# Pair sums and gated products carried across FFN tiles, and three convolution parts issued later in the mix

## The chip, the cores and the metric

The kernel runs on one core of one Trainium2 chip, as one launch. The metric is the device time of that launch in microseconds. The time before is the median of three runs.

A core has engines that run side by side, each with a queue of its own that it works through in order: PE (TensorE, the matrix multiplier), DVE (VectorE), ACT (ScalarE), POOL (GpSimd) and SP (SyncE), which here issues the loads of the weights. Matmul results land in PSUM, and DVE or ACT take them from there to SBUF. An instruction that waits for another engine holds up all that stand behind it in its own queue.

## What is computed

The reference is one inference step of a decoder trunk of two layers, for a prompt of 512 tokens and 8 samples of one token each. The kernel holds all 520 tokens as columns. Cut to what matters:

```python
def swiglu_ffn(x, wg, wu, wd):
    return (jax.nn.silu(x @ wg) * (x @ wu)) @ wd          # 1024 -> 2816 -> 1024

def layer(x, ...):
    x = x + 0.5 * swiglu_ffn(rms_norm(x, ffn1_norm), ffn1_wg, ffn1_wu, ffn1_wd)
    h = rms_norm(x, mix_norm)
    z = h @ w_in                                           # split into the inputs below
    o_r = rms_norm(retention(rq, rk, rv, ret_s), ret_norm_g) * jax.nn.silu(rg)   # 4 heads
    o_a = swa_attention(q, k, v, ...)                      # 4 query heads, window 128, sinks
    o_c = conformer_conv(ca, cg, conv_buf, ...)            # taps, layer norm, silu, then y @ pw
    x = x + jnp.concatenate([o_r, o_a, o_c], axis=-1) @ w_out
    x = x + 0.5 * swiglu_ffn(rms_norm(x, ffn2_norm), ffn2_wg, ffn2_wu, ffn2_wd)
    return x, ...                                          # and the new states and windows
```

## The kernel before

**Products in two parts.** A float32 value is kept as a high part and a low part in PE's float32r format. ACT makes the high part by a copy (`split_hi`, L290), DVE the low part by a subtraction (`split_lo`, L296), and each product is three matmuls (L334 and L342): high by low, high by high, low by high.

**The FFN.** The 2816 hidden channels are 22 tiles of 128. For each tile the gate product and the up product are formed over all 1024 inputs, then `gated` takes Silu of the gate half (L434) and multiplies (L436). There are two ways to form a tile:

- A *chunk* tile (`hidden`): 16 groups of matmuls (L342) with the weights as they are. DVE scales the gate half (L448) and the up half (L454).
- A *paired* tile (`pair_hidden`, the numbers in PAIRED): a fast multiplication scheme of two-by-two blocks, with seven block products (a11, s1, s2, a12, s3, s4, a22) in place of eight. `seven` issues them, 12 matmuls each (L334: four blocks, three matmuls for each). Products s1, s2 and s4 need sums of weight blocks, which DVE forms in place (`sums`: L258 for s1, L260 and L261 for s2, L263 for s4), into two slots of the tile Rd. Between products ACT copies an accumulator to the place where the next product adds to it: L528 copies c22 after a11, and product s2 waits for it.

The down projections are formed for groups of hidden tiles: group 0 (tiles 0 to 7) after hidden tile 8, group 1 (tiles 8 to 15) after hidden tile 16, group 2 (16 to 21) at the end. Groups 0 and 1 use the paired scheme (`pair_down`), whose right-hand sides are two hidden tiles and four sums of their halves: `pair_blocks` copies and splits the halves (ACT L509, DVE L512 three times), forms the four sums (`sums4`, DVE L461 to L464), copies them (ACT L480 twice) and splits them (DVE L484 twice).

**What sets the order.** All queues are filled in program order. The work of `gated`, `pair_blocks` and the other generators goes into a list `waiting`; `advance` runs the next piece, up to its `yield`. `seven` calls it after each product, seven times for a tile, and `hidden` after every second group, eight times. `flush` runs all that is left; it is called after every hidden tile and before each down projection. The weights come through four raw buffers of 512 KB; `load` issues the next DMA on SP when a buffer is free, which is when the last split of its products is done. `ahead` runs before each product: it makes casts as far ahead as the buffers of the split weights reach, then the subtractions, and after a product (not after a chunk) the sums of the next two products.

**The mix.** Its steps (input projection tiles, retention, attention, convolution, output projection) are generators as well, and a table ORDER written out by hand says which of them makes its next step. `cv` is the convolution: its last three steps are the product with pw (24 matmuls in two halves, into two PSUM tiles), the two high parts (ACT L774) and the two low parts (DVE L777). `n0` to `n3` are the norms of the four retention heads (column sums on PE L361, ACT L375 to L377, DVE L379, L380 and L1162), `g0` to `g3` the products with their gates (DVE L1178, split by ACT L1181 and DVE L1183), `s0` to `s3` the attention blocks of the prompt (scores on PE L867, DVE L852, ACT L879 to L888, transposes on PE L894, the copy L899, the product L906), `sa` the attention of the samples (PE L934). `kv` updates the retention state (PE L1051). The output projection (L342 again) follows.

PSUM is one pool of four tiles; each `ptile()` takes the next, and its first matmul waits until the last reader of the tile's previous content is done:

```python
    psum = pool("psum", 4, space=bass.MemoryType.PSUM)
```

Of the kernel before, what the change touches and what calls it, by code (L numbers as in the profile page):

```python
# [87 lines left out]

ORDER = """
CG0 al nrm h nrm pw l nrm pw h nrm l nrm CG0 rd RK0 CG0 CA0 h RK0 l CA1 CA0 h CG0 t l t t t CG1 t h t l t t t t CA1 t  # L90
RV1 h CG1 t CG1 l t t t t RV2 h t t RV1 l t t t t RV3 t RV1 h t RV2 l t t t t t RK1 h l t RV3 RV2 t ts ts RV1 RK1 t h
l RV2 RV1 RK1 RK1 RV2 RQ0 RK1 CG1 t t t t RQ0 t t h t l t t t t RQ1 RV3 RV0 h RQ1 qr l t t t t t RG0 t h t RV0 l t t t
RG0 t t RV0 AQ0 h t RG0 l t t t t AQ1 h AQ0 l t t RV0 h RV3 AQ1 RV3 RV0 t ri2 t AQ1 rv ri0 rv AQ1 RK0 cv ri0 AQ0 AQ0
rl AK0 AQ1 cv ri2 AQ1 rs0 cv RK0 rs0 AQ1 l h rs1 AV0 l rs1 AK0 AK0 RG1 h AK0 AV0 l AV0 rm RG1 h RG1 l AQ0 rm rm cv AQ0
RG2 AQ0 cv qs cv RG3 h RG2 cv l RG2 cv h RG3 AV0 RG3 cv AV0 RK0 kv cv kv cv kv AK0 l AK0 ri2 AK0 AK0 ri0 ri2 s1 ri0 n0
n2 s1 n1 n0 n3 s0 n3 n2 s0 n0 n1 n0 s3 s1 g0 n2 s1 n1 n2 g0 s1 n1 g2 n3 g1 s1 g1 g0 n3 g3 s0 s1 sa s2 g2 s3 g1 g3 s3
s1 s1 g2 g3 s0 s0 s1 sa a0 s3 s3 s2 a1 sa a0 s2 sa a2 a1 h s2 s2 l s3 a2 a3 s3 sa s3 a3 h sa s0 l s3 sa s0 s3 s0 sa s0
s2 a4 s0 s2 a5 a4 a6 a5 sa h s2 a6 a7 s2 s2 b0 l h l b1 b0 b0 b1 b0 b0 b2 h b0 b1 b1 b2 b1 b2 b1 b2 b3 l b4 h b3 b3 l
b2 b3 b5 b4 b3 b2 b4 b3 b4 b6 h b5 b5 l b4 b5 b7 a7 b6 b5 b4 b5 b6 b6 b7 b6 b7 b6 b7 b7 b7
""".split()  # L100


# [34 lines left out]
def step_kernel(ctx: ExitStack, tc: tile.TileContext, io: dict):  # L137
# [66 lines left out]
    seq, slot = [], [0]  # L204
# [14 lines left out]
    chunk = [0]  # L219
# [95 lines left out]
    def next_tile(look=True):
        u, c = at
# [122 lines left out]
    def hidden(norm, first):  # L439

        og, ou = ptile(), ptile()
        for i, (o, k) in enumerate(ffn_tiles(first, og, ou)):
            mm3(o, next_tile(), xh[:, k], xl[:, k], k == 0, k == KD - 1)
            if i % 2:
                advance()
            if i + 1 == KD and not first:
                t = wt("t")
                nc.vector.tensor_mul(v2(t), og[:, :, :HN], v2(R))  # L448
        if first:
            run(norm)  # L450
# [3 lines left out]
        nc.vector.tensor_mul(v2(u), ou[:, :, :HN], v2(R))  # L454
        return t, u, None
# [19 lines left out]

    def sum_parts(th, tl, u, w):
        sums4(u, w)
        yield
        for i, src in enumerate((u, w)):
            nc.scalar.copy(th[:, i * NT : (i + 1) * NT], src)  # L480
# [18 lines left out]
    def pair_blocks(u, w, spare, hs):  # L499
# [81 lines left out]
    def ffn(l, name, norm, after):  # L581
        hs, even, spare, xs = {n: [] for n in range(len(GROUPS))}, None, [], []
        for step, n in ffn_steps():
            if step == "hidden":
                g = next(i for i, (a, b, _) in enumerate(GROUPS) if a <= n < b)
                t, u, v = pair_hidden(xs) if n in PAIRED else hidden(norm, n == 0)
                flush()
                waiting.append(gated(t, u, v))
                if GROUPS[g][2] and n % 2:
                    waiting.append(pair_blocks(even, u, spare, hs[g]))  # L590
# [3 lines left out]
                    waiting.append(two_parts(u, hs[g]))  # L594
                waiting.extend(input_sums(l, name, j, xs) for j in {0: (0,), 1: (1, 2), 2: (3,)}.get(n, ()))
                continue
            flush()
            if GROUPS[n][2]:
                for m in range(0, KD, 2):
                    pair_down(m, hs[n])  # L600
# [833 lines left out]
```

## Time and profile before

| | |
|---|---|
| median of 3 runs | 1906.71 us (1905.59 to 1906.8) |
| the profiled execution | 1903.99 us |
| its span, first to last instruction | 1902.2 us |
| mean granted PE clock | 0.989 |
| matmuls | 15182 |
| loads of weights (512 KB each) | 318, 3.6 us from issue to landing (median) |

All views are of the one profiled execution. A row of a timeline gives the start in us from the span's start, the duration, the engine, the line, the operation and its tiles, and in brackets how long the engine was idle before it and what it waited for. A row of the waits gives the same for all instructions of a line: total us, how often, the longest. A line with `x12` joins as many like instructions. PE's granted clock is 1.00 at full speed.

### The profile page before, as it was taken

Reading aid. Unit: us, or ns where it says so; the run is one execution under the profiler, and the core shown is the slowest. Engines: PE = TensorE matmul, PEld = TensorE weight load, DVE = VectorE, ACT = ScalarE, POOL = GpSimd, SP = SyncE. Lnnn points to the kernel's source line nnn. Section 1 sums busy time; section 2 is a strip of 40 time slices with the busy share of each in tenths; the row PEclk is TensorE's granted clock in tenths of the full one; section 3 lists DMA queues with packets and bytes.
Section 4 is the critical chain, followed back from the end, with each engine's and each line's share of the span. In section 5 each row is a group of like instructions: output and inputs, shape, how many; then the busy total and the mean of one; then the engine's idle time right before and its main releaser. Section 6 shows DMA issues by size and latency. Waiting matters only on the chain.

```text
span 1902.2 us, 37220 instructions
## 1 busy us (share of the span) xinstructions
PE 1845.5 (97%) x15182; PEld 1821.8 (96%) x15182; DVE 1552.9 (82%) x2587; ACT 1051.3 (55%) x2052; POOL 23.3 (1%) x52
## 2 busy tenths in 40 slices
PE   8999999999999999999999999999998999999999
PEld 8999999999989999999999999999998999999999
DVE  8988888688667989888779888876886579889984
ACT  6655646533765656645555556565237556466452
POOL 0000000000100000000000000000000000000000
PEclk9999999999999999999999999999999999999999
DMA  5233224433312233323323232434333132333332
GB/s 182 79 100 112 90 89 127 129 104 115 117 43 92 78 90 100 102 88 107 116 80 100 87 92 89 124 114 125 101 113 105 45 100 68 95 108 100 92 96 90
DMA packets 54173, 189.37 MB, mean 100 GB/s; under 512 B 6273, under 2 KB 7153, under 8 KB 54001
## 3 DMA queue, kind: packets, MB, share of 16 engines
q1 hardware_dynamic: 50784, 177.35, 30.8%
q0 software_dynamic: 3072, 9.53, 1.5%
q8 instruction: 119, 1.95, 0.4%
q14 instruction: 54, 0.43, 0.1%
q10 hardware_dynamic: 144, 0.11, 0.0%
HBM read 179.50 MB, written 7.45 MB: 98 GB/s over the span
## 4 chain that ended last, share of the span: by engine, by line
PE 68%; DVE 20%; ACT 5%; issue 4%; DMA 3%; DVEq 0%; ACTq 0%; POOL 0%; POOLq 0%
PE o L342 37%; PE o L334 29%; DVE wl L296 4%; DVE wh L296 3%; DMA w<-in_w 2%; DVE m L484 2%; DVE u L436 1%; DVE m L512 1%; DVE u L431 1%; DVE w L260 1%; DVE t L431 1%; DVE t L429 1%; PE o L361 1%; ACT wh L290 1%; DVE u L462 1%
## 5 line engine op out<-in xcount | busy, mean ns | idle before, releaser
L342 PE MATMUL o<-xl,wh 128*128 128x260 f32 x1920 | 389.8, 284 | 6.5 <-DVE xl L387 6.0
L342 PE MATMUL o<-xh,wl 128*128 128x260 f32 x1920 | 387.6, 284 | 0.9 <-DVE wl L296 0.9
L342 PE MATMUL o<-xh,wh 128*128 128x260 f32 x1920 | 387.4, 283 | 0.0
L334 PE MATMUL o<-m,wh 128*128 128x260 f32 x2592 | 352.9, 286 | 16.8 <-ACT o L528 15.5
L290 ACT CAST wh<-w 128x1024 fp32r<-128x1024 f32 (+1 forms) x318 | 261.4, 822 | 193.3 <-PE o L342 134.9
L334 PE MATMUL o<-m,wl 128*128 128x260 f32 x2592 | 352.4, 285 | 16.2 <-ACT o L528 15.1
L334 PEld LDWEIGHTS o<-m,wh 128*128 128x128 f32 x2592 | 330.3, 191 | 20.9 <-ACT o L528 18.5
L334 PEld LDWEIGHTS o<-m,wl 128*128 128x128 f32 x2592 | 329.5, 190 | 20.0 <-ACT o L528 17.9
L342 PEld LDWEIGHTS o<-xl,wh 128*128 128x128 f32 x1920 | 297.4, 189 | 7.8 <-ACT wh L355 5.9
L342 PEld LDWEIGHTS o<-xh,wl 128*128 128x128 f32 x1920 | 297.1, 189 | 1.1 <-DVE wl L296 1.1
L342 PEld LDWEIGHTS o<-xh,wh 128*128 128x128 f32 x1920 | 296.6, 189 | 0.0
L296 DVE TENSOR_TENSOR wl<-w,wh 128x1024 fp32r<-128x1024 f32 x150 | 183.3, 1222 | 45.3 <-ACT wh L290 40.0
L342 PE MATMUL o<-m,wh 128*128 128x260 f32 x1024 | 164.5, 282 | 1.7 <-DVE m L520 1.7
L342 PEld LDWEIGHTS o<-m,wh 128*128 128x128 f32 x1024 | 140.0, 188 | 2.5 <-DVE m L520 2.5
L296 DVE TENSOR_TENSOR wh<-w,wh 128x512 fp32r<-128x512 f32 x168 | 115.1, 685 | 8.8 <-ACT wh L290 8.8
L296 DVE TENSOR_TENSOR wl<-w,wl 128x512 fp32r<-128x512 f32 x168 | 115.1, 685 | 8.7 <-ACT wl L290 8.7
L290 ACT CAST wl<-w 128x512 fp32r<-128x512 f32 x168 | 104.3, 621 | 30.0 <-PE o L334 16.1
L334 PE MATMUL o<-xh,wl 128*128 128x260 f32 x624 | 115.8, 283 | 0.0
L334 PE MATMUL o<-xh,wh 128*128 128x260 f32 x624 | 115.5, 282 | 0.0
L290 ACT CAST wl<-Rd 128x512 fp32r<-128x512 f32 x126 | 78.5, 623 | 59.6 <-PE o L334 27.8
L290 ACT CAST wh<-Rd 128x512 fp32r<-128x512 f32 x126 | 78.5, 623 | 57.5 <-PE o L334 26.3
L342 PE MATMUL o<-m,wl 128*128 128x260 f32 x512 | 102.7, 282 | 0.0
(219 smaller groups left out, 2674.7 us busy)
## 6 DMA issues: line engine op xcount, KB each, us to landing
w<-in_w SPq DMA_DIRECT2D x318, 512.0 KB, 3.6
out_y<-x SPq DMA_DIRECT2D x8, 260.0 KB, 2.0
m<-in_cm POOLq DMA_DIRECT2D x4, 512.0 KB, 4.2
m<-in_s_ret SPq DMA_DIRECT2D x4, 512.0 KB, 5.7
m<-sc POOLq DMA_DIRECT2D x8, 256.0 KB, 4.4
out_o_rets<-m POOLq DMA_DIRECT2D x4, 512.0 KB, 3.5
x<-in_x SPq DMA_DIRECT2D x3, 520.0 KB, 6.8
w<-in_w SPq DMA_DIRECT2D x4, 256.0 KB, 4.9
```

The costliest lines, as they stand in the source:

```text
L260: nc.vector.tensor_sub(a21, a21, a11)
L290: nc.scalar.copy(spl[u][0], source(u))
L296: nc.vector.tensor_sub(lo, source(u), h.bitcast(F32))
L334: nc.tensor.matmul(o, lhsT=a[:, s], rhs=b, start=first and j == 0 and i == 0, stop=j == JP - 1 and i == 2, skip_group_check=True,)
L342: nc.tensor.matmul(o[:, s, :HN], lhsT=a, rhs=b[:, s * HN : (s + 1) * HN], start=first and i == 0, stop=last and i == 2,)
L361: nc.tensor.matmul(o[:, s, :HN], lhsT=w, rhs=v[:, s * HN : (s + 1) * HN], start=i == 0, stop=i == len(parts) - 1,)
L429: nc.vector.tensor_add(d[:, HN:], d[:, HN:], v)
L431: nc.vector.tensor_mul(d, d, R)
L436: nc.vector.tensor_mul(u, u, t)
L462: nc.vector.tensor_sub(b12, b12, b11)
L484: nc.vector.tensor_sub(tl[:, c], src, th[:, c].bitcast(F32))
L512: nc.vector.tensor_sub(lo, a, h.bitcast(F32))
```

## The change

Four parts; nothing is removed from the computation and no instruction is added, only their order in the queues changes.

1. `ffn`: `flush` after a hidden tile is called only for tiles below the first paired one. What is left in `waiting` then goes on in the next tile. Before a paired down projection all but the last generator (the `gated` of the newest tile, which that projection doesn't use) are flushed; the last is put back and goes on during the projection.
2. `hidden`: `advance` is called after every group of matmuls, not every second, as long as more than two generators wait.
3. `pair_blocks` and `sum_parts`: an extra `yield` ahead of `sums4` and one behind it, so the work takes six calls instead of four.
4. `ahead`: after a product the sums are made for up to three of the next products, stopping at a pair of raw buffers that isn't loaded yet, and at an s1 while an s4 waits for its split, since both use slot 0 of Rd.

And in the mix the last three `cv` steps stand later in ORDER, among the steps of the norms and of the attention.

```diff
@@ ORDER (lines left out stand as they are) @@
-RG2 AQ0 cv qs cv RG3 h RG2 cv l RG2 cv h RG3 AV0 RG3 cv AV0 RK0 kv cv kv cv kv AK0 l AK0 ri2 AK0 AK0 ri0 ri2 s1 ri0 n0
+AQ0 cv qs cv RG3 h RG2 cv l RG2 cv h RG3 AV0 RG3 AV0 RK0 kv kv kv AK0 l AK0 ri2 AK0 AK0 ri0 ri2 s1 ri0 n0 n2 s1 n1 n0
+n3 s0 n3 n2 s0 n0 n1 n0 s3 s1 g0 n2 s1 n1 n2 g0 s1 n1 cv g2 n3 g1 s1 g1 cv g0 n3 g3 cv s0 s1 sa s2 g2 s3 g1 g3 s3 s1 s1
...
@@ def ahead @@
             split_lo()
         else:
             split_lo(old)
-            sums(nxt[0])
-            sums(nxt[0] + 1)
+            for v in range(nxt[0], min(nxt[0] + 3, len(seq))):
+
+                load()
+                if seq[v][0] != "chunk" and seq[v][1] + 1 >= loaded[0]:
+                    break
+                if seq[v][0] == "s1" and any(seq[p][0] == "s4" for p in pending):
+                    break
+                sums(v)
@@ def hidden @@
             mm3(o, next_tile(), xh[:, k], xl[:, k], k == 0, k == KD - 1)
-            if i % 2:
+            if i % 2 or len(waiting) > 2:
                 advance()
@@ def sum_parts @@
         sums4(u, w)
         yield
+        yield
         for i, src in enumerate((u, w)):
@@ def pair_blocks @@
         for (h, lo), a in zip(b, src):
             nc.vector.tensor_sub(lo, a, h.bitcast(F32))
+        yield
         yield from sum_parts(th, tl, u, w)
@@ def ffn @@
                 t, u, v = pair_hidden(xs) if n in PAIRED else hidden(norm, n == 0)
-                flush()
+                if n < PAIRED[0]:
+                    flush()
                 waiting.append(gated(t, u, v))
...
+            rest = [waiting.pop()] if GROUPS[n][2] else []
             flush()
+            waiting.extend(rest)
             if GROUPS[n][2]:
                 for m in range(0, KD, 2):
                     pair_down(m, hs[n])
```

Lines of the changed kernel lie a few further down, by 6 to 11: L460, L467 to L470, L491 and L442 are L454, L461 to L464, L484 and L436 of before; L385, L788, L863, L878, L905 and L945 are L379, L777, L852, L867, L894 and L934.

The queue of DVE at the end of hidden tile 8, first FFN, where the first down projection begins. Before:

```order
L464 TENSOR_TENSOR u<-u 128x260
L484 TENSOR_TENSOR m<-u,m 128x520 x2
L454 TENSOR_TENSOR u<-o,R 128x520
L436 TENSOR_TENSOR u<-u,t 128x520
L263 TENSOR_TENSOR Rd<-w,Rd 128x512
L296 TENSOR_TENSOR wl<-w,wl 128x512
L296 TENSOR_TENSOR wh<-Rd,wh 128x512
L258 TENSOR_TENSOR Rd<-w 128x512
```

And in the changed kernel, from the same sum on:

```order
L470 TENSOR_TENSOR u<-u 128x260
L460 TENSOR_TENSOR u<-o,R 128x520
L491 TENSOR_TENSOR m<-u,m 128x520 x2
L263 TENSOR_TENSOR Rd<-w,Rd 128x512
L296 TENSOR_TENSOR wl<-w,wl 128x512
L296 TENSOR_TENSOR wh<-Rd,wh 128x512
L258 TENSOR_TENSOR Rd<-w 128x512
L260 TENSOR_TENSOR w<-w 128x512
L261 TENSOR_TENSOR Rd<-w 128x512
L442 TENSOR_TENSOR u<-u,t 128x520
```

The scaling of the up half comes before the splits of the pair sums, and the gated product of the tile (L436, now L442) goes behind the next sums L258 to L261; L263 has one operation less in front of it since the sums.

The same queue at the end of hidden tile 12, where paired tile 13 begins. Before:

```order
L464 TENSOR_TENSOR u<-u 128x260
L484 TENSOR_TENSOR m<-u,m 128x520 x2
L454 TENSOR_TENSOR u<-o,R 128x520
L263 TENSOR_TENSOR Rd<-w,Rd 128x512
L296 TENSOR_TENSOR wh<-w,wh 128x512
L296 TENSOR_TENSOR wl<-Rd,wl 128x512
L258 TENSOR_TENSOR Rd<-w 128x512
L436 TENSOR_TENSOR u<-u,t 128x520
```

In the changed kernel:

```order
L470 TENSOR_TENSOR u<-u 128x260
L460 TENSOR_TENSOR u<-o,R 128x520
L263 TENSOR_TENSOR Rd<-w,Rd 128x512
L491 TENSOR_TENSOR m<-u,m 128x520 x2
L296 TENSOR_TENSOR wh<-w,wh 128x512
L296 TENSOR_TENSOR wl<-Rd,wl 128x512
L258 TENSOR_TENSOR Rd<-w 128x512
L260 TENSOR_TENSOR w<-w 128x512
L261 TENSOR_TENSOR Rd<-w 128x512
```

Here L263 passes the two splits of the pair sums (L484, now L491) as well.

The queue of PE in the mix of layer 0, from the column sums of the norms to the output projection; the numbers tell the PSUM tiles `o` apart. Before:

```order
L361 MATMUL o_6192<-rsq_6184,one128_118 128x260 x2
L361 MATMUL o_6195<-rsq_6171,one128_118 128x260 x2
L361 MATMUL o_6210<-rsq_6179,one128_118 128x260 x2
L867 MATMUL o_6217<-m_6141,m_5718 128x256 x4
L894 MATMUL o_6261<-cc_85,m_6173 128x128 x8
L934 MATMUL o_6285<-m_4602,m_4606 32x128 x8
L867 MATMUL o_6295<-m_6141,m_5718 128x256 x4
```

In the changed kernel, where o_6221 and o_6234 are the two halves of the product with pw:

```order
L367 MATMUL o_6160<-rsq_6152,one128_118 128x260 x2
L367 MATMUL o_6163<-rsq_6139,one128_118 128x260 x2
L367 MATMUL o_6178<-rsq_6147,one128_118 128x260 x2
L878 MATMUL o_6185<-m_6109,m_5718 128x256 x4
L348 MATMUL o_6221<-m_6014,pwh_4549 128x260 x2
...
L348 MATMUL o_6234<-m_6013,pwl_4550 128x260 x2
L905 MATMUL o_6255<-cc_85,m_6141 128x128 x8
L945 MATMUL o_6285<-m_4602,m_4606 32x128 x8
L878 MATMUL o_6295<-m_6109,m_5718 128x256 x4
```

The pw product now stands between the last scores and the transposes; in the program before it stood ahead of L1051. The queue of DVE at the same place, from the fourth norm on, before:

```order
L379 SCALAR_TENSOR_TENSOR nt_6256<-o_6192,epst_86,nt_6256 128x520
L380 SCALAR_TENSOR_TENSOR rr_6254<-nt_6256,y0_6255 128x520
L1162 SCALAR_TENSOR_TENSOR m_5879<-m_5879,par_84,rr_6254 128x520
L1178 TENSOR_TENSOR m_6011<-m_6011,m_5879 128x520
L852 ISA m_6301,st_6216<-o_6217,m_4164,nsink_120 128x256
```

In the changed kernel:

```order
L385 SCALAR_TENSOR_TENSOR nt_6250<-o_6160,epst_86,nt_6250 128x520
L386 SCALAR_TENSOR_TENSOR rr_6248<-nt_6250,y0_6249 128x520
L1173 SCALAR_TENSOR_TENSOR m_5879<-m_5879,par_84,rr_6248 128x520
L1189 TENSOR_TENSOR m_6011<-m_6011,m_5879 128x520
L788 TENSOR_TENSOR m_6266<-o_6221,m_6265 128x520
L788 TENSOR_TENSOR m_6266<-o_6234,m_6265 128x520
L863 ISA m_6301,st_6184<-o_6185,m_4164,nsink_120 128x256
```

The two low parts of the pw product (L777, now L788) stand behind the fourth norm's gate product and ahead of the last scores' reduction, and they are the last readers of the PSUM tiles o_6221 and o_6234.

More of the change, by code (lines that the diff above doesn't have):

```diff
@@ L90 @@
 CG0 al nrm h nrm pw l nrm pw h nrm l nrm CG0 rd RK0 CG0 CA0 h RK0 l CA1 CA0 h CG0 t l t t t CG1 t h t l t t t t CA1 t
[L91 to L94, printed above, removed]
-RG2 AQ0 cv qs cv RG3 h RG2 cv l RG2 cv h RG3 AV0 RG3 cv AV0 RK0 kv cv kv cv kv AK0 l AK0 ri2 AK0 AK0 ri0 ri2 s1 ri0 n0
[L96 to L99, printed above, removed]
+RV1 h CG1 t CG1 l t t t t RV2 h t t RV1 l t t t t RV3 t RV1 h t RV2 l t t t t t RK1 h l t RV3 RV2 t ts ts RV1 RK1 t h l
+RV2 RV1 RK1 RK1 RV2 RQ0 RK1 CG1 t t t t RQ0 t t h t l t t t t RQ1 RV3 RV0 h RQ1 qr l t t t t t RG0 t h t RV0 l t t t
+RG0 t t RV0 AQ0 h t RG0 l t t t t AQ1 h AQ0 l t t RV0 h RV3 AQ1 RV3 RV0 t ri2 t AQ1 rv ri0 rv AQ1 RK0 cv ri0 AQ0 AQ0 rl
+AK0 AQ1 cv ri2 AQ1 rs0 cv RK0 rs0 AQ1 l h rs1 AV0 l rs1 AK0 AK0 RG1 h AK0 AV0 l AV0 rm RG1 h RG1 l AQ0 rm rm cv AQ0 RG2
+AQ0 cv qs cv RG3 h RG2 cv l RG2 cv h RG3 AV0 RG3 AV0 RK0 kv kv kv AK0 l AK0 ri2 AK0 AK0 ri0 ri2 s1 ri0 n0 n2 s1 n1 n0
+n3 s0 n3 n2 s0 n0 n1 n0 s3 s1 g0 n2 s1 n1 n2 g0 s1 n1 cv g2 n3 g1 s1 g1 cv g0 n3 g3 cv s0 s1 sa s2 g2 s3 g1 g3 s3 s1 s1
+g2 g3 s0 s0 s1 sa a0 s3 s3 s2 a1 sa a0 s2 sa a2 a1 h s2 s2 l s3 a2 a3 s3 sa s3 a3 h sa s0 l s3 sa s0 s3 s0 sa s0 s2 a4
+s0 s2 a5 a4 a6 a5 sa h s2 a6 a7 s2 s2 b0 l h l b1 b0 b0 b1 b0 b0 b2 h b0 b1 b1 b2 b1 b2 b1 b2 b3 l b4 h b3 b3 l b2 b3
+b5 b4 b3 b2 b4 b3 b4 b6 h b5 b5 l b4 b5 b7 a7 b6 b5 b4 b5 b6 b6 b7 b6 b7 b6 b7 b7 b7
 """.split()
```

## The prediction

> **What bounds the kernel now.** I read the page's first part, then the waits of each engine, then the timelines around the longest waits, then the windows for the clock.
>
> ```profile
> PE 1845.5 (97%) x15182; PEld 1821.8 (96%) x15182; DVE 1552.9 (82%) x2587; ACT 1051.3 (55%) x2052; POOL 23.3 (1%) x52
> PE o L334 <- ACT o L528: 30.6, 13, 3.0
> PE o L894 <- ACT m L888: 9.3, 2, 4.6
> ```
>
> The first row says that TensorE is busy for 1845.5 of 1902.2 us. The change removes no matmul, so it can win only the 56.7 us in which PE has none, and whatever PE loses to a lower clock. The second and third rows (engine, line and what it waited for: total us, times, longest) name the two largest parts of that idle time: 30.6 us before the accumulator copy L528 in the FFNs, and 9.3 us before the softmax transposes L894 in the mixes. The change touches both places.
>
> The 30.6 us are in effect twelve stalls, three in each of the four FFNs. Eight of them follow hidden tiles 8 and 16, when the down projection begins (type A); four follow hidden tile 12, when paired tile 13 begins (type B). Here is a type A stall: DVE, then ACT, then PE (start us, duration, what it did, and in brackets the idle time before).
>
> ```profile
> 110.40 0.43 DVE L464 TENSOR_TENSOR u<-u 128x260 f32<-128x260 f32 x1
> 111.05 1.31 DVE L484 TENSOR_TENSOR m<-u,m 128x520 fp32r<-128x520 f32 x2 [0.23 <-ACT m L480]
> 112.28 0.69 DVE L454 TENSOR_TENSOR u<-o,R 128x520 f32<-128x520 f32 x1
> 113.08 0.70 DVE L436 TENSOR_TENSOR u<-u,t 128x520 f32<-128x520 f32 x1
> 113.70 0.68 DVE L263 TENSOR_TENSOR Rd<-w,Rd 128x512 f32<-128x512 f32 x1
> ...
> 110.40 1.16 ACT L480 CAST m<-u 128x520 fp32r<-128x520 f32 x2 [3.25 <-DVE u L463]
> 114.42 0.62 ACT L290 CAST wh<-Rd 128x512 fp32r<-128x512 f32 x1 [1.82 <-DVE Rd L263]
> 114.94 0.37 ACT L528 COPY o<-o 128x260 f32<-128x260 f32 x1
> ...
> 109.39 1.59 PE L334 MATMUL o<-m,wl 128*128 128x260 f32 x12
> 110.81 1.62 PE L334 MATMUL o<-m,wh 128*128 128x260 f32 x12
> 115.36 1.71 PE L334 MATMUL o<-m,wl 128*128 128x260 f32 x12 [2.93 <-ACT o L528]
> ```
>
> PE does the products a11 and s1 and then needs the copy of a11's accumulator (L528). That copy is only 0.37 us, and its input was ready at about 110.8; it runs at 114.94 because it stands in ACT's queue behind the cast L290 of a weight sum. That cast waits 1.82 us for the sum itself, L263, and L263 is the fifth row of a DVE queue that has no gap to give. So the wait is named after L528, but its cause is **where L263 stands on DVE**.
>
> The type B stall is alike, without the gated product L436 in the row:
>
> ```profile
> 196.38 0.43 DVE L464 TENSOR_TENSOR u<-u 128x260 f32<-128x260 f32 x1
> 197.04 1.31 DVE L484 TENSOR_TENSOR m<-u,m 128x520 fp32r<-128x520 f32 x2 [0.23 <-ACT m L480]
> 198.27 0.69 DVE L454 TENSOR_TENSOR u<-o,R 128x520 f32<-128x520 f32 x1
> 198.88 0.68 DVE L263 TENSOR_TENSOR Rd<-w,Rd 128x512 f32<-128x512 f32 x1
> ...
> 199.65 0.62 ACT L290 CAST wl<-Rd 128x512 fp32r<-128x512 f32 x1 [1.59 <-DVE Rd L263]
> ...
> 200.59 1.58 PE L334 MATMUL o<-m,wh 128*128 128x260 f32 x11 [2.19 <-ACT o L528]
> ```
>
> **The FFN stalls, worked out.** Type A: in the new order L454 comes right after L464, and L436 goes behind L263 and L261. L464 starts at 110.40 and takes 0.43, so L454 can start at 110.8 (its tile was complete at 109.39, when PE went on). From one start to the next L454 costs 0.61 (198.27 to 198.88), the two L484 cost 1.23 (197.04 to 198.27), and the wait of 0.23 for L480 falls under L454. L263 then starts at 110.8 + 0.61 + 1.23 = 112.65 instead of 113.70: 1.05 us earlier. The rest of the chain keeps its lengths, and PE's stall ends 1.05 earlier. Eight of these give 8.4 us. What is late next is still L263, behind the pair sums.
>
> Type B: the new order puts both L484 behind L263. Only L454 stands between, so L263 starts at 196.8 + 0.61 = 197.4 instead of 198.88. ACT has by then done L480 and one more cast (196.38 + 1.16 + about 0.6 = 198.1) as L263 ends at 198.1, so its queue doesn't take the gain back. Gain 1.48 each, four of them 5.9 us. Sum of the FFN stalls: **-14.3 us**. Bounds: nothing, if another row of the same queue takes L263's place, and -30.6, if the whole wait goes.
>
> The extra steps, the advances that come twice as often and the missing flush at paired tiles shift Silu, copies and splits later. I cost them at nothing: their consumers are a tile away, and what covers them is PE's work of such a tile, seven products of twelve matmuls at 1.42 us each (109.39 to 110.81), about 10 us. Were the cover gone, each would show as a DVE or ACT row of 0.4 to 0.7 us in front of L334.
>
> **A DVE wait that moves.** Before each of the twelve stalls DVE also waits for weights:
>
> ```profile
> 93.60 0.69 DVE L296 TENSOR_TENSOR wh<-w,wh 128x512 fp32r<-128x512 f32 x1
> 94.81 1.22 DVE L296 TENSOR_TENSOR wl<-w,wh 128x1024 fp32r<-128x1024 f32 x1
> 98.23 0.69 DVE L258 TENSOR_TENSOR Rd<-w 128x512 f32<-128x512 f32 x1 [2.20 <-DMA w<-in_w]
> ...
> 90.06 0.62 ACT L290 CAST wh<-w 128x512 fp32r<-128x512 f32 x1
> ...
> DVE Rd L258 <- DMA w<-in_w: 20.8, 10, 2.3
> ```
>
> The subtraction at 93.60 frees the buffer, SP issues the load, and L258 starts when it has landed, 3.9 us after the subtraction's end at 94.3. In the new order that subtraction goes ahead of the two L429 and the two L431 (as large as L464 and L436 above, so about 2 us together), and its cast was done at 90.7; but L436 and the split at 94.81 (0.70 + 1.22) go behind L258. So the load starts about 1.9 earlier, L258 comes due 1.9 earlier, and the wait, 10 times 2.1 us by the last row, stays. Sum zero; bounds -2 and +2 us for each of the twelve. Behind L258 are L260, L261 and the splits of the next products, which ACT and PE wait for.
>
> **The clock.**
>
> ```profile
> 112.50:115.30 2.80, 0.00 (x0) 1.00 0.02 6
> 115.40:119.00 3.60, 3.60 (x30) 1.00 0.63 180
> ...
> 243.00:246.30 3.30, 0.38 (x4) 1.00 0.00 0
> 246.90:250.30 3.40, 3.40 (x18) 0.50 0.82 217
> ...
> 1642.95:1646.35 3.40, 3.40 (x18) 0.50 0.72 253
> ...
> 1191.55 59.26 PE o L334 x480
> 1773.50 58.02 PE o L334 x480
> ```
>
> These rows give a window in us, PE's busy time and matmuls, and the granted clock. The stall at 112.5 left the clock at 1.00; the one at 243 is followed by 3.4 us at half clock. What that costs is in the last two rows, from the chain: 480 matmuls took 59.26 with such a stretch and 58.02 without, so 1.24 us. Six of the twelve stalls have such a stretch behind them (the first at 246.9, the last at 1642.95): five of type A (about 3 us each), one of type B (about 2). With type A cut to about 2 us I expect them to behave as type B does now, one in four, and type B, cut to 0.7, not at all: two stretches remain, and four times 1.24 gives **-5.0 us**; bounds 0 and -7.4. The Trainium skill ("TensorE: Matmul & The Clock Gate", Part 1) has the clock drop after at least one idle window of about 3.4 us. By that no stall of this kernel's FFNs would lower it and this term would be 0; the rows above speak against it, since 3.3 us with 0.38 us of work in them were enough.
>
> **The mix.** All times are from layer 0; layer 1 repeats them.
>
> ```profile
> 507.16 1.97 PE L1051 MATMUL o<-m 128*64 128x128 f32 x32
> 527.48 1.97 PE L894 MATMUL o<-cc,m 128*128 128x128 f32 x8 [4.63 <-ACT m L888]
> 529.38 3.62 PE L934 MATMUL o<-m 128*32 128x128 f32 x16
> 535.55 0.50 PE L342 MATMUL o<-xl,wh 128*128 128x260 f32 x2
> ...
> 504.46 0.68 DVE L985 TENSOR_TENSOR m<-o,rt 128x512 f32<-128x512 f32 x1
> 507.89 0.70 DVE L777 TENSOR_TENSOR m<-o,m 128x520 fp32r<-128x520 f32 x1 [0.30 <-ACT m L774]
> 530.86 0.75 DVE L379 SCALAR_TENSOR_TENSOR nt<-o,epst,nt 128x520 f32<-128x520 f32 x1
> 533.17 0.70 DVE L1178 TENSOR_TENSOR m<-m 128x520 f32<-128x520 f32 x1
> ```
>
> Taking the pw matmuls away from before L1051 brings L1051 forward to where its input is ready (L985 ends at 505.14, so about 505.2): -1.96 us for the whole chain behind it. Their new place is after the last scores L867 and before L894, in the 4.63 us that PE waits there; that looks free. But the program has four PSUM buffers, and at that place all four are held: three by sums for the norms, one by the scores. In the new order the pw matmuls wait for L379 of the second and third norm, L894 waits for L379 of the fourth (530.86 + 0.75 = 531.6 instead of 527.48), and L934, next behind it on PE, needs the buffer of the first pw half, which the first L777 frees. L777 stands on DVE behind L1178 of the fourth norm: 533.17 + 0.70 + 0.70 = 534.6. So L934 starts at 534.6 instead of 529.38, 5.2 later. From there to the output projection before it is 535.55 - 529.38 = 6.17 us, at half clock; at full clock 3.1. The projection starts at 540.7 or at 537.7, less 1.96 for the earlier chain: 538.8 or 535.7, against 535.55. That is +3.2 or +0.15 us for each layer; I take the middle, since PE's gaps there are broken up by the pw matmuls but not filled: **+3.4 us** for both layers. Bounds: -3.9 (if only the 1.96 counts) and +10.4 (if none of it does). Behind L934 are L867, L906 and the whole projection.
>
> **The sum.** -14.3 - 5.0 + 3.4 = -15.9 us. The profiled execution took 1903.99 (span 1902.2), so 1888.1 by that measure; the median of the runs is 2.7 us higher, 1906.71, so **1891** there.
>
> **The rivals.**
>
> *The clock does not follow the stalls.* Windows run at times of their own, and the shorter stalls may still lower the clock as often. Then the clock term is 0 and the sum -10.9: 1896. For it: three of the eight type A stalls left the clock alone, the one at 112.5 among them, and one of type B did not, so it is phase as much as length. Chance 0.15.
>
> *The mix gains.* If PSUM does not bind as worked out, the pw matmuls are hidden in the wait and each layer keeps its 1.96: -14.3 - 5.0 - 3.9 = -23.2, 1883.5; with the rest of the FFN stalls also going, down to 1870. For it: 4.63 us of idle PE against about 3 us of matmuls. Against it: four buffers, and the norms that hold them end only at 531.6. Chance 0.18.
>
> *It does not do what it says.* The sums stay behind the same queue, as L258's wait and the 82% busy DVE leave no room; FFN 0, mix +3.4: 1910, or about 1904 with a part of the clock term. Chance 0.10.
>
> *Slower: L258's wait goes to the wrong side.* If the freeing subtraction is held where it is (its cast L290 comes from an ACT queue that the change also alters), the load still lands at 98.2, and now L436 and the 1024-wide split stand behind the wait and not in front of it. Then each of the twelve stalls is 1.9 us later against 1.05 or 1.48 gained: 8 x 0.85 + 4 x 0.42 = +8.5, with the mix +11.9: 1918.6. It decides from a delay of (14.3 + 5.0 - 3.4) / 12 = 1.3 us at each place. Against it: that cast ends 2.9 us before the subtraction starts now. Chance 0.09.
>
> **How the numbers follow.** The forecast, 1886 to 1896 with its own size errors, has 0.48; the rivals above have the chances named. The range runs from 1874 to 1907: it takes in the first rival, most of the second, where a larger part of the FFN's wait goes, and half of the third. A measurement of this kernel can tell about 0.2%, 3.8 us, from no change. Faster by more than that: the forecast, the first two rivals, and a part of the third, 0.83. Within: 0.09. Slower: 0.08.
>
> **What would show it.** In the trace after: L454 directly behind L464, and L263 about 1 us earlier at the first stall of each FFN; the wait of L334 for L528 at about 16 us in all, near 1.9 for type A and 0.7 for type B; two half-clock stretches in the FFNs in place of six; DVE's wait for w at L258 about 20 us still. In the mix, L1051 about 2 us earlier, L894 waiting for L379, L934 for L777, and the output projection 0 to 3 us later than now. The forecast is wrong if a different row holds L528 back, if L258's wait doubles, or if L894 still ends its wait with L888.

## The result and the profile after

| | before | after |
|---|---|---|
| median | 1906.76 us (4 runs) | 1894.17 us (4 runs, 1891.72 to 1896.72) |
| ratio | | 0.9937, 95% interval 0.992 to 0.9954 |
| the profiled execution | 1903.99 us | 1895.39 us |
| its span | 1902.2 us | 1893.6 us |
| mean granted PE clock | 0.989 | 0.993 |

The forecast was 1891, the measured median 1894.2: 12.6 us faster instead of 15.9. Lines of the changed kernel are a few higher, as in the section on the change (L348, L340 and L536 are L342, L334 and L528). The waits of PE after, and one row of DVE's:

```profile
PE o L340 <- ACT o L536: 18.1, 16, 1.6
PE o L348 <- DVE wl L296: 9.6, 13, 1.9
...
DVE Rd L258 <- DMA w<-in_w: 35.7, 16, 2.9
```

The wait for the accumulator copy fell from 30.6 to 18.1 us. The second row is new: PE waits for the low part of a weight, twelve times in the chunk tiles and once in the mix. DVE's wait for weights at L258 looks as if it had grown from 20.8 (10 times) to 35.7 (16 times). But before, the profile puts two of the twelve waits down to `issue`:

```profile
DVE Rd L258 <- issue: 4.1, 2, 2.2
```

So it was 24.9 us at twelve places, and at these twelve it is 24.8 after. The other 10.9 us are four new waits, one in each FFN (the first at 299.26, 2.87 us), behind which PE does not stop.

The type A stall of the first FFN after, DVE, then ACT, then PE:

```profile
110.77 0.43 DVE L470 TENSOR_TENSOR u<-u 128x260 f32<-128x260 f32 x1
111.12 0.69 DVE L460 TENSOR_TENSOR u<-o,R 128x520 f32<-128x520 f32 x1
111.73 1.30 DVE L491 TENSOR_TENSOR m<-u,m 128x520 fp32r<-128x520 f32 x2
112.95 0.68 DVE L263 TENSOR_TENSOR Rd<-w,Rd 128x512 f32<-128x512 f32 x1
...
114.19 0.37 ACT L536 COPY o<-o 128x260 f32<-128x260 f32 x1
...
114.61 1.59 PE L340 MATMUL o<-m,wl 128*128 128x260 f32 x11 [1.51 <-ACT o L536]
```

From the last pair sum to L263 it is now 2.18 us (110.77 to 112.95) and was 3.30 (110.40 to 113.70): 1.12 less, in the order shown with the change. PE's wait fell by more, from 2.93 to 1.51, because PE now comes to this place 0.67 us later (its wait begins at 113.10 and began at 112.43). PE had lost 0.80 us at tile 5, shown below, and 0.39 us in the chunk tile 14 us earlier; short waits that went gave back about 0.5. The chunk tile:

```profile
92.50 0.69 DVE L296 TENSOR_TENSOR wh<-w,wh 128x512 fp32r<-128x512 f32 x1
...
94.40 0.69 DVE L437 TENSOR_TENSOR u<-u,R 128x520 f32<-128x520 f32 x1
96.86 0.69 DVE L258 TENSOR_TENSOR Rd<-w 128x512 f32<-128x512 f32 x1 [1.77 <-DMA w<-in_w]
97.47 1.22 DVE L296 TENSOR_TENSOR wl<-w,wh 128x1024 fp32r<-128x1024 f32 x1
...
98.74 0.51 PE L348 MATMUL o<-xh,wl 128*128 128x260 f32 x2 [0.23 <-DVE wl L296]
```

The subtraction at 92.50 frees the buffer, L258 waits for its load, and behind it stands the 1024-wide split, which now starts at 97.47 and started at 94.81 before. PE needs its result at once. The third such place of this FFN costs 1.56 us, counted from one matmul's start to the next.

Type B, where L263 passed both splits:

```profile
196.11 0.69 DVE L460 TENSOR_TENSOR u<-o,R 128x520 f32<-128x520 f32 x1
196.72 0.68 DVE L263 TENSOR_TENSOR Rd<-w,Rd 128x512 f32<-128x512 f32 x1
...
198.45 1.58 PE L340 MATMUL o<-m,wh 128*128 128x260 f32 x11 [0.50 <-ACT o L536]
```

The wait fell from 2.19 to 0.50. Tile 5 has a new stall: from one matmul's start to the next it is 1.25 us there, where it was 0.45 in the first FFN and 0.12, so none, in the others (DVE and PE after):

```profile
60.88 0.70 DVE L454 TENSOR_TENSOR t<-o,R 128x520 f32<-128x520 f32 x1 [0.96 <-PE o L348]
...
68.74 0.68 DVE L263 TENSOR_TENSOR Rd<-w,Rd 128x512 f32<-128x512 f32 x1
...
70.46 1.71 PE L340 MATMUL o<-m,wh 128*128 128x260 f32 x12 [0.97 <-ACT o L536]
```

Before, DVE did the pair sums while the scaling of the gate half waited for PE; now they come behind that scaling, DVE sits idle for 0.96 us, and L263 is late (68.02 before).

The mix of layer 0 after (PE, then DVE):

```profile
503.10 1.97 PE L1062 MATMUL o<-m 128*64 128x128 f32 x32 [0.94 <-DVE m L996]
521.31 1.24 PE L348 MATMUL o<-m,pwh 128*128 128x260 f32 x4 [2.58 <-DVE nt L385]
527.54 1.09 PE L905 MATMUL o<-cc,m 128*128 128x128 f32 x8 [1.64 <-DVE nt L385]
530.46 1.91 PE L945 MATMUL o<-m 128*32 128x128 f32 x16 [1.82 <-issue]
534.44 0.51 PE L348 MATMUL o<-xl,wh 128*128 128x260 f32 x2
...
529.67 1.30 DVE L788 TENSOR_TENSOR m<-o,m 128x520 fp32r<-128x520 f32 x2
```

PE enters this stretch 2.19 us earlier than before. The first product L1062 (L1051 of before) is 4.06 earlier, the pw product waits for a norm, the transposes wait for the fourth norm and are 0.06 later than before, L945 starts after the first L788 and is 1.08 later, and the projection starts 1.11 earlier. So the stretch loses 1.08 us; in layer 1 by the same matmuls 2.69.

The clock after (window, PE busy and matmuls, granted clock):

```profile
244.50:247.90 3.40, 3.40 (x30) 1.00 0.51 154
483.70:490.40 6.70, 6.70 (x25) 0.50 0.54 159
```

The first window follows the third stall of the first FFN, which before had half clock behind it. In this trace none of the FFNs has such a stretch any more; the mixes still have them, as the second window shows.

When the start-to-start gap in front of each matmul is compared between the two traces, the change divides so (us, both profiled executions):

| | forecast | measured |
|---|---|---|
| type A stalls, 8 | -8.4 | -10.5 |
| type B stalls, 4 | -5.9 | -5.8 |
| half clock behind the FFN's stalls | -5.0 | -8.9 |
| waits in the chunk tiles, 12 | 0 | +9.7 |
| stall at tile 5, 4 | 0 | +4.2 |
| short waits between paired products, and the rest of the FFNs | 0 | -5.2 |
| mix, from L834 to the projection | +3.4 | +3.8 |
| mix, ahead of that | 0 | +4.1 |
| sum | -15.9 | -8.6 |

The first two rows and the waits in the chunk tiles and at tile 5 belong together: 16.3 us of PE's stalls went and 13.9 came back at other places of the same tiles, so 2.4 us are left of them.

-8.6 is the difference of the two profiled executions; the medians differ by 12.6, since the one of before lies 2.7 below its median and the one after 1.2 above.

### The profile page after: what moved, and what is told of

Read it like the earlier page. It is cut to its first block, busy times and chain, and to the rows that moved or that the text cites. A ratio compares the mean times of both kernels' runs of the same rounds, so it can differ in the third digit from the quotient of the medians.

```text
span 1893.6 us, 37172 instructions
## 1 busy us (share of the span) xinstructions
PE 1839.3 (97%) x15182; PEld 1816.5 (96%) x15182; DVE 1558.1 (82%) x2587; ACT 1051.6 (56%) x2052; POOL 23.4 (1%) x52
## 4 chain that ended last, share of the span: by engine, by line
PE 74%; DVE 15%; ACT 4%; DMA 3%; issue 3%; SPq 0%; DVEq 0%; POOL 0%; ACTq 0%
PE o L348 37%; PE o L340 35%; DVE wl L296 4%; DMA w<-in_w 2%; DVE wh L296 2%; DVE m L491 2%; DVE u L442 1%; PE o L367 1%; DVE m L519 1%; DVE w L260 1%; DVE t L437 1%; ACT t L440 1%; DVE Rd L263 0%; ACT wh L290 0%; ACT wl L290 0%
## 5 line engine op out<-in xcount | busy, mean ns | idle before, releaser
L348 PE MATMUL o<-xh,wl 128*128 128x260 f32 x1920 | 389.2, 284 | 9.6 <-DVE wl L296 9.6
L348 PE MATMUL o<-xl,wh 128*128 128x260 f32 x1920 | 390.1, 284 | 5.7 <-DVE xl L393 5.7
L348 PE MATMUL o<-xh,wh 128*128 128x260 f32 x1920 | 387.7, 284 | 0.0
L340 PE MATMUL o<-m,wl 128*128 128x260 f32 x2592 | 347.9, 283 | 9.1 <-ACT o L536 8.9
L340 PE MATMUL o<-m,wh 128*128 128x260 f32 x2592 | 347.6, 283 | 9.2 <-ACT o L536 9.2
L340 PEld LDWEIGHTS o<-m,wl 128*128 128x128 f32 x2592 | 325.9, 188 | 11.6 <-ACT o L536 10.5
L340 PEld LDWEIGHTS o<-m,wh 128*128 128x128 f32 x2592 | 325.6, 188 | 11.6 <-ACT o L536 10.9
L348 PEld LDWEIGHTS o<-xh,wl 128*128 128x128 f32 x1920 | 297.2, 189 | 12.4 <-DVE wl L296 12.4
L348 PEld LDWEIGHTS o<-xl,wh 128*128 128x128 f32 x1920 | 297.9, 190 | 6.9 <-ACT wh L361 5.7
L348 PEld LDWEIGHTS o<-xh,wh 128*128 128x128 f32 x1920 | 296.9, 189 | 0.0
L348 PE MATMUL o<-m,wh 128*128 128x260 f32 x1024 | 164.6, 282 | 1.7 <-DVE m L528 1.7
L348 PEld LDWEIGHTS o<-m,wh 128*128 128x128 f32 x1024 | 140.0, 188 | 2.5 <-DVE m L528 2.5
L340 PE MATMUL o<-xh,wl 128*128 128x260 f32 x624 | 115.5, 282 | 0.0
L340 PE MATMUL o<-xh,wh 128*128 128x260 f32 x624 | 115.5, 282 | 0.0
L440 ACT ACTIVATE t<-t 128x520 f32<-128x520 f32 x88 | 56.1, 638 | 94.0 <-DVE t L437 93.7
```

What stands on the lines that cost most here:

```text
L340: nc.tensor.matmul(o, lhsT=a[:, s], rhs=b, start=first and j == 0 and i == 0, stop=j == JP - 1 and i == 2, skip_group_check=True,)
L348: nc.tensor.matmul(o[:, s, :HN], lhsT=a, rhs=b[:, s * HN : (s + 1) * HN], start=first and i == 0, stop=last and i == 2,)
L440: nc.scalar.activation(t, t, AF.Silu)
```

## The experiments

Each was timed in five rounds against the kernel before; ratios are to that kernel. Every program has line numbers of its own, a few off: in the rows, L530, L532 and L536 are the copy L528 of before, L442 is L436 and L486 is L484; L905 and L899 of ffn_only are L894 and L888; L1056, L990 and L899 of late_cv are L1051, L985 and L894.

**order_only.** The program of before with the new ORDER.

```diff
-RG2 AQ0 cv qs cv RG3 h RG2 cv l RG2 cv h RG3 AV0 RG3 cv AV0 RK0 kv cv kv cv kv AK0 l AK0 ri2 AK0 AK0 ri0 ri2 s1 ri0 n0
+AQ0 cv qs cv RG3 h RG2 cv l RG2 cv h RG3 AV0 RG3 AV0 RK0 kv kv kv AK0 l AK0 ri2 AK0 AK0 ri0 ri2 s1 ri0 n0 n2 s1 n1 n0
...
```

> The program of before with only the new table ORDER (the three convolution parts late in the mix), the FFN as before. Theory 1, four PSUM buffers: the fourth norm's L379 and then L777 hold L894 and L934, each layer's output projection starts 1.0 to 2.7 us later counted from the product L834, the sum over both layers is +3.6 us, so about 1910 us. Theory 2, the pw product is hidden in the wait before L894: each layer keeps the 1.9 us by which L1051 comes forward, -3.8 us, about 1903 us. The trace tells them apart also without the time: under theory 1 L894 waits for L379 and L934 waits after it, under theory 2 L894 waits for L888 as before.

Measured: 1907.83 us, ratio 1.002 (1.0009 to 1.0031), so +3.8 us with 1.7 to 5.9 as the interval. Its waits of PE:

```profile
PE o L894 <- DVE nt L379: 4.7, 2, 2.3
PE o L934 <- issue: 2.8, 2, 1.8
```

L894 waits for the norm and L934 waits behind it, so theory 1 holds. From L834 to the output projection the trace has 34.15 and 34.24 us in the two layers, 31.46 and 31.47 before: +2.7 each, with half clock in that stretch in both. The changed kernel has 32.55 in layer 0, at full clock from L945 on, and 34.16 in layer 1. The four other programs with the new ORDER at this place (two_sums, no_yields, flush_only, no_far_s1) show the same two sizes: a layer costs 1.1 us, or 2.6 to 2.9, by where half clock falls in the stretch.

**ffn_only.** The changed program with the old ORDER.

> The changed program with the old ORDER. Theory 1: the mix parts cost 3.6 us, so 1894.2 - 3.6 = 1890.6 us. Theory 2: they gain 3.8 us, so about 1898 us. In both the FFN stalls stay as in the changed program: about 18 us of L334 waiting for the accumulator copy and about 10 us of L342 waiting for the low part in the chunk tiles.

Measured: 1887.63 us, ratio 0.9915 (0.9901 to 0.9929), and L905 waits for the softmax again:

```profile
PE o L340 <- ACT o L536: 17.3, 16, 1.6
PE o L348 <- DVE wl L296: 9.4, 13, 2.1
PE o L905 <- ACT m L899: 9.3, 2, 4.6
```

The FFN parts alone bring 0.85%, the whole change 0.63%: the mix part takes a quarter of it back.

**two_sums.** The changed program with the old rule for the sums.

```diff
-            for v in range(nxt[0], min(nxt[0] + 3, len(seq))):
...
-                sums(v)
+            sums(nxt[0])
+            sums(nxt[0] + 1)
```

> The changed program with the old rule for weight sums (the next two products, no look at what is loaded), everything else new. Theory A, the waits of the chunk tiles are a cost of the longer look ahead: the 9.7 us of L342 waiting for L296 go, the 5 us of short waits between paired products that the look ahead had removed come back, about -5 us, 1889. Theory B, DVE's queue from the load of the weights to L263 sets the end and PE only waits at one place or the other: the waits of L342 go, those of L334 for the accumulator copy grow by nearly as much (from 18 to 26 us or more), and the short waits come back as well, so 1894 to 1900.

Measured: 1870.29 us, ratio 0.982 (0.9806 to 0.9834): neither. It is 24 us faster than the whole change by the medians and 22 by the ratios; theory A allowed 5. DVE and, at the end, PE's waits:

```profile
92.15 0.68 DVE L296 TENSOR_TENSOR wh<-w,wh 128x512 fp32r<-128x512 f32 x1
...
94.65 1.21 DVE L296 TENSOR_TENSOR wl<-w,wh 128x1024 fp32r<-128x1024 f32 x1
95.79 0.69 DVE L436 TENSOR_TENSOR u<-u,t 128x520 f32<-128x520 f32 x1
96.45 0.69 DVE L258 TENSOR_TENSOR Rd<-w 128x512 f32<-128x512 f32 x1
...
PE o L334 <- ACT o L530: 10.8, 12, 1.5
```

L258 has no wait left at this place, and 3.8 us in the whole program. The buffer is freed as early as in the changed kernel, and six operations (L429 and L431 twice each, the split, L436) fill the time in which the load lands. The wait at L258 stood ahead of everything up to L263 in a queue without a gap, so it came back at PE: from the chunk tile to the stall PE takes 1.2 to 2.9 us less at each of the twelve places, 21 us in all between the two traces. Both theories had left that wait as given.

**no_yields.** The changed program without the two extra pauses.

```diff
         sums4(u, w)
         yield
-        yield
...
-        yield
         yield from sum_parts(th, tl, u, w)
```

> The changed program without the two extra pauses around the pair sums. At hidden tile 12 the splits of the pair sums (L484 of before) stand ahead of L263 again, at tiles 8 and 16 ahead of the scaling L454 but without the gated product; at hidden tile 4 the pair sums stand ahead of the scaling of the gate half again. If the pauses are what moved L263 at tile 12: those four stalls return to about 2.1 us (+5.6), those of tiles 8 and 16 grow by the 0.3 us wait for the casts (+2.4), the four new stalls of 1.25 us at tile 5 go (-3.4 to -4.2), and one or two half-clock stretches return (+1 to +2.5): +5 us, about 1899. If instead the longer look ahead moved L263, nothing but tile 5 changes: -4 us, 1890.

Measured: 1908.0 us, ratio 1.0016 (1.0008 to 1.0025), 14 us slower than the whole change where +5 was expected. The stall at tile 5 went as expected, but DVE's wait grew:

```profile
DVE Rd L258 <- DMA w<-in_w: 49.9, 16, 3.6
...
92.31 0.69 DVE L437 TENSOR_TENSOR u<-u,R 128x520 f32<-128x520 f32 x1
93.53 0.68 DVE L296 TENSOR_TENSOR wh<-w,wh 128x512 fp32r<-128x512 f32 x1
97.90 0.69 DVE L258 TENSOR_TENSOR Rd<-w 128x512 f32<-128x512 f32 x1 [3.08 <-DMA w<-in_w]
```

So the pauses do more than move L263. The calls that they use up push the first piece of the next `gated` (L429 and L431 of before, here L435 and L437, twice each) behind the subtraction that frees the buffer; without them that piece is done before it, at 92.31, and no longer covers the load.

**look_only.** The program of before with only the long look ahead.

> The program of before with only the new rule for weight sums (up to three products ahead). Theory: L258 now stands ahead of the gated product and the 1024-wide split, but the subtraction that frees the buffer stays behind, so each of the twelve waits of DVE for the load grows from about 2 us to 3.5 to 4, and everything up to L263 is 1.5 to 1.9 us later: +18 to +23 us, less the short waits between paired products (about -5): 13 to 18 us slower than before. Rival, the look ahead is harmless by itself and hurts only together with the missing flush: within 5 us of before.

Measured: 1916.4 us, ratio 1.0055 (1.0041 to 1.0068), +11 us, just under the 13 to 18 expected. In its trace the half-clock stretches in the FFNs also cost 4 us less, which the expectation left out. At the first place of DVE:

```profile
93.84 0.69 DVE L296 TENSOR_TENSOR wh<-w,wh 128x512 fp32r<-128x512 f32 x1
94.45 0.70 DVE L442 TENSOR_TENSOR u<-u,t 128x520 f32<-128x520 f32 x1
98.45 0.69 DVE L258 TENSOR_TENSOR Rd<-w 128x512 f32<-128x512 f32 x1 [3.30 <-DMA w<-in_w]
```

**flush_only.** The changed program with the old rule for the sums and without the pauses.

> The changed program with the old rule for weight sums and without the two extra pauses, so of the FFN only the missing flush and the advances. To be compared with two_sums (1870). If the pauses act through the place of L263 alone (the splits L484 ahead of it at tile 12, the wait of 0.3 us for the casts at tiles 8 and 16), they are worth 8 us at those twelve places and cost 4 us at tile 5: about 1874. If they are worth what they were with the long look ahead (14 us), about 1884.

Measured: 1895.16 us, ratio 0.9944 (0.9931 to 0.9958): 25 us slower than two_sums, more than either value. Its row for L258 is nearly that of before (and again two of the twelve waits, 4.1 us, stand under `issue`):

```profile
DVE Rd L258 <- DMA w<-in_w: 20.9, 10, 2.5
```

The pauses are thus worth 25 us with the short look ahead, their harm at tile 5 already taken off. Six programs form one series. From the end of the freeing subtraction to L258 it is 3.6 to 3.9 us in all of them, and how much DVE does in that time sets its wait (first chunk tile behind a pair, first FFN):

| program | between the subtraction and L258 | wait of L258 there | all such waits | time |
|---|---|---|---|---|
| look_only | L436 | 3.30 | 49.9 | 1916.4 |
| no_yields | L436 | 3.08 | 49.9 | 1908.0 |
| before | L436, split | 2.20 | 24.9 | 1905 to 1907 |
| flush_only | L436, split | 1.94 | 25.0 | 1895.2 |
| after | L429 and L431 twice each | 1.77 | 35.7 | 1894.2 |
| two_sums | L429 and L431 twice each, split, L436 | none | 3.8 | 1870.3 |

**no_far_s1.** The changed program; the look ahead stops before an s1 that is three products away.

```diff
+                if seq[v][0] == "s1" and v > nxt[0] + 1:
+                    break
```

> The changed program with the long look ahead, except that it stops before the first sum (s1, L258) of a pair that is three products away. In this order L258 stands behind the 1024-wide split and the gated product again, as in two_sums; all other sums stay where the change put them. If L258's wait for its load is the whole harm of the look ahead: no wait of L258 (under 2 us in all), no wait of L342 for the split, 1868 to 1872 as two_sums. If the earlier second and third sums or the earlier loads cost something too, between 1875 and 1894.

Measured: 1872.2 us, ratio 0.9826 (0.9813 to 0.984), and

```profile
DVE Rd L258 <- DMA w<-in_w: 4.1, 9, 0.9
```

Of all that the long look ahead moves, L258 alone does the harm. The other earlier sums cost nothing that can be measured, and bring nothing either.

**two_sums_old_order.** two_sums with the old ORDER.

> two_sums with the old ORDER. The FFN parts and the mix are separate stretches of the program, so the gain of the one adds to the other: 1870.3 less the 3.8 us that ORDER cost alone is 1866.5. If the FFN's gain hid some of ORDER's cost (or the half-clock stretches in the mix depend on it), 1870 to 1872.

Measured: 1865.48 us, ratio 0.9788 (0.9775 to 0.9802). The parts add.

**late_cv.** two_sums with the convolution parts moved on into the output projection.

```diff
-n3 s0 n3 n2 s0 n0 n1 n0 s3 s1 g0 n2 s1 n1 n2 g0 s1 n1 cv g2 n3 g1 s1 g1 cv g0 n3 g3 cv s0 s1 sa s2 g2 s3 g1 g3 s3 s1 s1
...
+g3 s0 s0 s1 sa a0 s3 s3 s2 a1 sa a0 s2 sa a2 a1 h s2 s2 l s3 a2 a3 s3 sa s3 a3 h cv sa s0 l s3 sa cv s0 s3 s0 sa s0 s2
+a4 cv s0 s2 a5 a4 a6 a5 sa h s2 a6 a7 s2 s2 b0 l h l b1 b0 b0 b1 b0 b0 b2 h b0 b1 b1 b2 b1 b2 b1 b2 b3 l b4 h b3 b3 l
```

> two_sums with the three convolution parts still later, in the output projection, where PE has work without a gap and PSUM tiles turn over fast. Theory 1 (PSUM): L1051 comes forward by 1.9 us per layer as in the changed program, L894 waits for L888 again and not for L379, and the pw product costs its 2.9 us of PE there as it did at the old place: 3.8 us better than two_sums_old_order, 1862 to 1863. If what holds the projection back is not the buffers but DVE and ACT in that stretch, no better than the old place: 1866 or more.

Measured: 1864.11 us, ratio 0.9786 (0.9772 to 0.98): the same as two_sums_old_order. The waits came as theory 1 has them, but its price was wrong:

```profile
493.37 1.97 PE L1056 MATMUL o<-m 128*64 128x128 f32 x32 [0.93 <-DVE m L990]
...
535.57 0.74 PE L342 MATMUL o<-m,pwh 128*128 128x260 f32 x4
...
538.54 0.60 PE L899 MATMUL o<-cc,m 128*128 128x128 f32 x4
```

The stretch from L834 to the projection fell to 29.5 us in both layers (31.5 with the product at its old place). But in the projection, where PE has no idle time for it to fill, the pw product costs its whole 2.97 us (535.57 to 538.54). At its old place it costs only the 1.9 us by which L1051 comes forward without it, since PE would else have waited 0.9 us for L985. The old place hides a third of it, and moving it out wins nothing: by the trace each layer loses 1.1 us. The time does not show this loss, because ahead of that stretch the mixes of its trace are 3.0 us shorter than in two_sums_old_order, which has a half-clock stretch there in each layer (mean clock 0.994 against 0.998).

**tile5.** two_sums_old_order, with the pauses only for pairs from hidden tile 5 on.

```diff
-        yield
+        if late:
+            yield
...
-                    waiting.append(pair_blocks(even, u, spare, hs[g]))
+                    waiting.append(pair_blocks(even, u, spare, hs[g], n >= PAIRED[0]))
```

> two_sums_old_order, with the two extra pauses only for pairs of hidden tiles from 5 on. At hidden tile 4 the pair sums stand ahead of the scaling of the gate half again, so DVE does them while it would else wait about 1 us for PE, and L263 of tile 5 comes 0.7 us earlier: the four stalls of 1.25 us at tile 5 fall to the 0.12 to 0.45 us of the program before, -3 to -4.5 us, 1861 to 1862.5. If DVE's queue is bound elsewhere by then, the stall only moves: 1865.

Measured: 1858.99 us, ratio 0.9758 (0.9744 to 0.9773): by the ratios about 6 us less than two_sums_old_order, somewhat more than expected. The four stalls at tile 5 do what was forecast: 1.25 us from start to start became 0.12 to 0.18, 4.5 us in all; the rest is not traced to a cause. What is left of the wait for the copy are the eight type A stalls:

```profile
PE o L334 <- ACT o L532: 7.2, 8, 1.6
```

**sum_first.** tile5 without the flush before the paired projections, so that L263 passes the splits there too.

```diff
-            rest = [waiting.pop()] if GROUPS[n][2] else []
-            flush()
-            waiting.extend(rest)
+            if not GROUPS[n][2]:
+                flush()
```

> tile5, and nothing is flushed before the paired down projections, so that L263 stands ahead of the last splits of the pair sums (L484) at hidden tiles 8 and 16 as it does at tile 12. L263 is then 1.2 us earlier there; the stall that is left is 1.0 us (two_sums: gaps of 0.94 to 1.0 us, PE's own pitch 0.12), so about 0.9 goes at each of eight places, -7 us against tile5, about 1854. What is late next could be the splits L484, which the second product s1 needs for its fourth block: if they are, PE stops up to 0.5 us inside s1 and the gain is half, 1857 to 1858.

Measured: 1854.51 us, ratio 0.9737 (0.9724 to 0.9751), the fastest. DVE and PE at the place of the first type A stall:

```profile
108.44 0.70 DVE L454 TENSOR_TENSOR u<-o,R 128x520 f32<-128x520 f32 x1
109.06 0.68 DVE L263 TENSOR_TENSOR Rd<-w,Rd 128x512 f32<-128x512 f32 x1
109.65 1.31 DVE L486 TENSOR_TENSOR m<-u,m 128x520 fp32r<-128x520 f32 x2
...
109.66 1.61 PE L334 MATMUL o<-m,wh 128*128 128x260 f32 x12
111.11 1.60 PE L334 MATMUL o<-m,wl 128*128 128x260 f32 x12
```

PE goes from s1 to s2 without a stop, 1.45 us from start to start. Between the two traces the eight type A stalls give 8.5 us; the medians differ by 4.5, where 7 were expected. It is 2.7% under the kernel before; the change as made kept 0.6%.

## Why the prediction was right, and where it was not

**The FFN stalls.** The step from the order to the stall held: L263 was late because of its place, and it came forward by 1.12 us at type A (1.05 forecast), and at type B, where L454 alone stands ahead of it since the last pair sum, PE's wait fell by 1.69 at the first place (1.48 forecast). That the size of the A term came out larger (-10.5) is the other side of the waits in the chunk tiles, which make PE late for that place (0.67 us at the first, with tile 5's). So the stalls were not won as the sum has it: 16.3 us went there where 14.3 were forecast, but with what came back in the chunk tiles and at tile 5 only 2.4 us are left.

**"Sum zero", the DVE wait that moves.** This step failed. The wait at L258 did stay, 24.9 us at the twelve places before and 24.8 after, but the text named the splits that now stand behind it and priced them at nothing; the 1024-wide split went from 94.81 to 97.47, and PE lost 9.7 us in the chunk tiles. More than that was hidden in the zero: it was a difference of two large terms. The missing flush and the pauses take nearly the whole wait away (two_sums, 3.8 us left), the long look ahead brings it back (no_far_s1 without, the whole change with it: 22 us). The prediction worked the two out together and so did not see that the change had a part that undoes another. The check in `ahead` did not guard against this: the section on the change says that the sums stop at buffers that aren't loaded yet, but the count `loaded` grows when a load is put into SP's queue, not when it has landed.

**Steps, advances and pauses "at nothing".** Failed at tile 5, +4.2 us; tile5 shows it, where the four stalls go with the pauses taken away (4.5 us in its trace). The cover named, PE's work of a tile, was that of a later tile, and the cost was DVE's: its queue met the scaling of the gate half before PE had finished it. In the other direction, 5.2 us of short waits between paired products went, which had no term.

**The clock.** The direction held, and the size was too small: all six stretches went (-8.9), not four (-5.0), and each was worth 1.5 us, not 1.24. That none was left is partly luck: ffn_only, with the same order in the FFNs, has one (at 230.6, behind a wait of 2.11 us in a chunk tile). By the rule of the Trainium skill ("TensorE: Matmul & The Clock Gate", Part 1) the term would have been nothing; the traces decide against it, since PE was busy for 1.53 of the 3.41 us ahead of the stretch at 1144.6 before.

**The mix.** Right in mechanism and in the sum of both layers: +3.4 forecast, +3.8 by the trace of the changed kernel and +3.8 in the time of order_only, through the fourth norm and L777. The two values worked out for a layer, +0.15 at full clock and +3.2 at half clock, stand against 1.1 and 2.7 measured. The way to L934 came out: with the 2.19 us by which PE enters the stretch taken off, L934 is 3.27 us later, and 5.2 - 1.96 = 3.24 was worked out. What was mis-sized is the 3.1 us from there to the projection at full clock; it took 3.98 (530.46 to 534.44). The prediction had halved all of the 6.17 us of before, but only the part up to 533.6 was at half clock. The rival in which the move gains is refuted by order_only. The 4.1 us ahead of that stretch, longer half-clock stretches and one wait for a DMA that is 1 us longer, were not forecast. The trace of order_only has the longer wait too (4.6 us, 3.5 before). The stretches need not be the change's: in the programs with the old ORDER the same part of a layer is between 1.7 us shorter (tile5) and 1.6 longer (look_only) than before, as half clock falls elsewhere. No run separates the two.

**The rivals.** The slower one named the right mechanism, L258 waiting ahead of what PE needs, but took its cause to be a subtraction that stays in place. That happens in look_only, and the kernel is then slower, by 11 us. In the change the pauses move the subtraction, as the text had it.

So that the total came close is in good part luck: what had no price (+12.8 in all) was nearly half made good by terms that came out larger than forecast (-5.5), of which 3.9 are the clock's; of the rest, 3.9 us is how the two profiled executions lie to their medians. The mechanism at the twelve stalls was right, the price of what was moved behind L258 was not, and most of the gain in the trace is half clock and short waits, not the stalls.

## What to carry to other kernels

In a queue that is full, look at each instruction that waits for a load: what stands between the event that starts the load and that instruction is its cover, and what stands behind it pays for the wait. An operation that is issued earlier gives up cover, so a look ahead should stop at operands that are still under way, not only at those whose load hasn't been issued. Time the parts of a bundled change one by one: here the missing flush, the more frequent advances and the pauses were worth 40 us without the long look ahead and the new ORDER (two_sums_old_order), and the long look ahead cost 22.

## What the runs showed of the hardware

Half clock came in stretches of 3.41 us or twice that, and within a trace all of them begin a whole number of 3.413 us apart (246.88, 489.22 and 526.77 before: 71 and 11 steps), so the moments at which one can begin are set by a fixed beat and not by the end of the stall. The longer PE's stalls at the twelve places, the more such stretches the FFNs of a trace have: 6 and 5 with type A stalls of about 3.1 us from start to start (before, order_only), 3 with 2.5 us (look_only), 2 with 2.1 to 2.4 us (flush_only), none or one with 1.8 us and less. No length of stall is seen to be safe. Of the four type B stalls before, one had half clock behind it (1144.4, 2.16 us) and three of 2.0 to 2.5 us had none; none of the eight type A stalls of about 1.8 us after did, but one of 1.80 us in tile5 (1.52 us of idle time) had:

```profile
238.90 2.14 PE L334 MATMUL o<-m,wl 128*128 128x260 f32 x12 [1.52 <-ACT o L532]
...
239.95:243.30 3.35, 3.35 (x18) 3.35 (x17) 3.32 (x7) 1.39 (x3) 0.00 (x0) 0.50 0.63 193
```

The second row gives a window, the busy time of PE, its weight loads, DVE, ACT and POOL, and then the clock: 0.50. In the 3.41 us ahead of it PE was busy for 1.87.

The runs after differ with the clock: 1891.72 us at a mean of 0.995, 1896.72 at 0.993. From the end of the freeing subtraction to the start of a waiting L258 it took 3.7 to 3.9 us at the first place in the five programs of the series that wait, whatever stood between.
